# A hybrid encoder layer on one core: the down projection's first two tile pairs of each chunk interleaved, and the sums of the next feed-forward rows spread over four blocks

## The chip, the cores and the metric

One core of a Trainium2 chip runs the whole program. The metric is the device time in microseconds of one execution, as the median of several. The engines are TensorE (PE in the profile, its weight loads PEld), VectorE (DVE), ScalarE (ACT), GpSimd (POOL) and SyncE (SP), which here only issues transfers. Each works through its own instructions in order.

## The reference

One layer of a streaming encoder on 2176 rows (2048 of a prompt, 8 x 16 of running streams; 17 tiles of 128 rows), 1024 wide. A first half (a gated delta rule on four heads and a short convolution, with projections) ends in `x = x + RMSNorm(mix)`. The change concerns the second half:

```python
h = rmsnorm(x, norm_ffn_pre)
f = (jax.nn.silu(h @ w_gate) * (h @ w_up)) @ w_down      # 1024 -> 2816 -> 1024
x = x + rmsnorm(f, norm_ffn_post)
```

All is float32. The kernel splits each operand in a high part (a rounded copy) and a low part (the rest) and multiplies high x high, high x low and low x high.

## The kernel before

**Products.** Both projections of the feed-forward use Strassen's scheme in Winograd's form: two by two blocks with seven products in place of eight, bought with sums and differences of blocks.

**Gate and up.** The 17 tiles stand in three groups (`FGROUPS`: six, six and five tiles). For each group the rows are loaded (`ffn_load`, tiles `fh`), summed (`ffn_sums`, lines L1158, L1159 and, from the second group on, L1162, tiles `ft`) and split (`ffn_prep`, tiles `xh`, `xl`). Then come 22 blocks `f`, one for each 128 columns of gate and up: `gu_start` makes the first four products in four banks, `gate_up` copies them out on ScalarE (L1288 to L1290), makes the other three and forms silu(gate) times up on VectorE (L1296 to L1317). Every second block ends in sums for the down projection (`pt`, L1323 to L1326), which ScalarE's queue sends to memory (`partd`, L1328). The split weights `fw` of the next block are made alongside (L1220 to L1230) or, for later groups, partly read back (`fsplit`). Rows of the next group are loaded behind blocks 4 to 11 of the running one; its sums stand behind block 16 (`NF - 6`).

**Down.** The 22 blocks are the inner dimension of the down projection, in five chunks (`FCHUNKS`: four blocks four times, six at the end). In each chunk, eight tile pairs (`down_pair`) and the half tile pair left over (`down_single`) are multiplied with the chunk's weights; `acc` collects the five chunks' results. A pair has seven parts (`ar`, loaded by SP from `partd` in pieces of two, two and three parts; three buffers). Each part is split (`split`: L1399 the copy on ScalarE, L1402 the difference on VectorE or GpSimd; tiles `as`, six buffers) and multiplied (`product`, L1418; 6 matmuls, 9 in the last chunk) into one of four banks, each of which takes a second product after its first was brought out. Bringing out (`evac`) is a copy on ScalarE in the first chunk (L1451) and an addition on VectorE after it (`acc_add`, L1377). The eight banks go round (`fbank`).

The weights are prepared by a generator, `down_chunk`, one step at a time (`prep_step`): raw rows `dr` (L1084, four buffers), differences on VectorE (L1091 to L1097), and splits in a ring of 21 tiles `dw` (one of them `sA`, `sB`; L1108 the copy on ScalarE, L1110 the difference on VectorE or GpSimd). In a chunk of 14 weights, seven of the next chunk's are made in the middle; the steps for the others stand in its last pair, and the ring passes into the chunk after.

In the last chunk each pair ends in two differences (L1477, L1478) and two calls of `finish` (norm and residual): sums of squares on ScalarE (L1427), products with the gain (L1431), then the row scale and the residual (L1436), and the output.

**Order.** The framework's scheduler runs over the program with a timeline of its own (`TLS = True`), so an engine's final order is near the program's but not the same. `tc.issue_after` sets a lower bound for single instructions.

## Time and profile before

| | us |
|---|---|
| Median of 3 runs | 2518.31 (2517.99 to 2518.65) |
| The profiled execution | 2521.97 |
| its span, first to last instruction | 2520.1 |
| TensorE busy | 2464.6 |
| VectorE busy | 1612.6 |
| ScalarE busy | 1063.8 |
| GpSimd busy | 588.1 |
| First product of the down projection starts | 2036.9 |
| Its last products (48 matmuls from 2496.4) end | 2507.5 |

In the timeline's rows stand the start and the duration in us, the engine, the line, the operation, output and inputs, shapes, how many in a row were merged, and in brackets the idle time just before and what ended it. A row of the waits has the waiting engine, tile and line, whom it waited for, the total in us, how often, and the longest. A row of the windows has the stretch and its length, then for each engine the busy time and the number of instructions, then TensorE's granted clock (1 is full speed), the share of the transfer engines and GB/s. In a row of the groups the busy time and the mean in ns of one stand behind the first bar, idle time behind the second.

### The profile page before, as it was taken

The page shows a single profiled execution, that of the slowest core. Times are in us where ns is not written, and L with a number is a line of the kernel's source. Part 1 is how long each engine was busy: PE and PEld are TensorE (multiplying, and loading weights), DVE is VectorE, ACT ScalarE, POOL GpSimd, SP SyncE. Part 2 cuts the span into 40 slices and gives each one's busy share as a digit, 9 for nine tenths or more (in the row PEclk, how much of TensorE's full clock was granted, in tenths as well). Part 3 has the DMA queues.
Part 4 walks back from the last instruction along what each step waited for, and adds up shares of the span by engine and source line. Part 5 has one row for each costly group of instructions (what it writes and reads, how often), then busy time and mean ns, then how long its engine had stood idle before and what let it go on. Part 6 is the DMA issues. An engine that isn't in the chain of part 4 may idle for free. (4 is left out here: it accounts for less than half of the span.)

```text
span 2520.1 us, 39370 instructions
## 1 busy us (share of the span) xinstructions
PE 2464.6 (98%) x14366; PEld 2253.3 (89%) x14366; DVE 1612.6 (64%) x3025; ACT 1063.8 (42%) x2355; POOL 588.1 (23%) x663
## 2 busy tenths in 40 slices
PE   8999999999999999999999999999999999999997
PEld 7988888889999988789999999999999987887786
DVE  5966645645666555868878754455555564677688
ACT  5656445445435343534444422223333345333343
POOL 1101011011010001325665400000000055455564
PEclk9999999999999999999999999999999999999999
DMA  7855555456676556669876878878998743344465
GB/s 268 320 205 193 211 194 193 176 181 225 231 243 235 196 187 223 222 227 322 293 273 239 284 246 277 268 246 262 290 308 282 255 146 121 93 126 124 129 222 184
DMA packets 282498, 561.91 MB, mean 223 GB/s; under 512 B 26108, under 2 KB 174784, under 8 KB 265024
## 3 DMA queue, kind: packets, MB, share of 16 engines
q1 hardware_dynamic: 161200, 483.52, 56.6%
q10 hardware_dynamic: 121104, 75.88, 9.6%
q8 instruction: 113, 1.85, 0.3%
q14 instruction: 81, 0.66, 0.1%
HBM read 400.62 MB, written 158.70 MB: 222 GB/s over the span
## 5 line engine op out<-in xcount | busy, mean ns | idle before, releaser
L1254 PE MATMUL fbank<-xh,fw 128*128 128x384 f32 (+1 forms) x3696 | 898.9, 326 | 4.5 <-DVE ht L1055 2.0
L298 PE MATMUL dbank<-hi,w 128*128 128x384 f32 (+1 forms) x2240 | 671.9, 368 | 8.9 <-ACT w L277 6.0
L1254 PEld LDWEIGHTS fbank<-xh,fw 128*128 128x128 f32 x3696 | 651.9, 188 | 5.8 <-ACT m L1290 2.6
L1254 PE MATMUL fbank<-xl,fw 128*128 128x384 f32 (+1 forms) x1848 | 602.5, 326 | 0.0
L298 PEld LDWEIGHTS dbank<-hi,w 128*128 128x128 f32 x2240 | 416.7, 190 | 48.2 <-ACT w L277 6.2
L1418 PE MATMUL fbank<-dw,as 128*128 128x512 f32 x1884 | 445.2, 395 | 8.0 <-DVE as L1402 2.8
L1418 PEld LDWEIGHTS fbank<-dw,as 128*128 128x128 f32 x1884 | 355.2, 189 | 91.8 <-DVE acc L1377 4.1
L298 PE MATMUL dbank<-lo,w 128*128 128x384 f32 (+1 forms) x1120 | 402.2, 359 | 1.1 <-DVE lo L216 1.1
L1254 PEld LDWEIGHTS fbank<-xl,fw 128*128 128x128 f32 x1848 | 347.4, 188 | 0.0
L1402 POOL TENSOR_TENSOR as<-ar,as 128x256 fp32r<-128x256 f32 (+1 forms) x207 | 186.4, 911 | 230.1 <-ACT as L1399 227.0
L298 PEld LDWEIGHTS dbank<-lo,w 128*128 128x128 f32 x1120 | 212.9, 190 | 18.7 <-DVE lo L216 1.6
L1377 DVE TENSOR_TENSOR acc<-acc,fbank 128x512 f32<-128x512 f32 x248 | 166.3, 682 | 97.5 <-PE fbank L1418 83.4
L1399 ACT CAST as<-ar 128x256 fp32r<-128x256 f32 (+1 forms) x288 | 118.6, 427 | 187.1 <-PE fbank L1418 133.8
L1110 POOL TENSOR_TENSOR dw<-dr,dw 128x512 fp32r<-128x512 f32 x48 | 70.2, 1473 | 521.5 <-ACT dw L1108 521.4
L1229 ACT CAST fw<-rg 128x512 fp32r<-128x512 f32 x124 | 77.3, 623 | 187.8 <-PE fbank L1254 158.9
L302 DVE SCALAR_TENSOR_TENSOR acc<-R,cw,acc 128x384 f32<-128x384 f32 (+2 forms) x180 | 121.6, 677 | 53.0 <-ACT acc L332 44.4
L1301 DVE TENSOR_TENSOR c<-u,fbank 128x384 f32<-128x384 f32 (+1 forms) x66 | 34.9, 529 | 116.0 <-PE fbank L1254 116.0
L1299 ACT ACTIVATE m<-fbank 128x384 f32<-128x384 f32 (+1 forms) x66 | 31.3, 474 | 132.8 <-PE fbank L1254 131.8
L1297 DVE TENSOR_TENSOR m<-m,m 128x384 f32<-128x384 f32 (+1 forms) x44 | 23.1, 525 | 92.1 <-ACT m L1290 92.0
L1230 POOL TENSOR_TENSOR fw<-rg,fw 128x512 fp32r<-128x512 f32 x44 | 68.6, 1558 | 45.0 <-ACT fw L1229 44.8
L324 POOL COPY hist<-R 128x3 f32<-128x3 f32 x60 | 18.3, 305 | 255.1 <-ACT R L307 202.1
L1290 ACT COPY m<-fbank 128x384 f32<-128x384 f32 (+1 forms) x66 | 30.5, 461 | 88.5 <-PE fbank L1254 57.0
(362 smaller groups left out, 3573.6 us busy)
## 6 DMA issues: line engine op xcount, KB each, us to landing
w<-wsplit SPq DMA_DIRECT2D x105, 1024.0 KB, 5.1
fw<-fsplit SPq DMA_DIRECT2D x188, 512.0 KB, 4.6
fsplit<-fw SPq DMA_DIRECT2D x94, 512.0 KB, 3.9
partd<-pt ACTq DMA_DIRECT2D x88, 384.0 KB, 6.3
rg<-in_w_gu SPq DMA_DIRECT2D x62, 512.0 KB, 3.6
wsplit<-w SPq DMA_DIRECT2D x28, 1024.0 KB, 4.9
ar<-partd SPq DMA_DIRECT2D x48, 384.0 KB, 3.3
wr<-in_w_in SPq DMA_DIRECT2D x34, 512.0 KB, 5.9
```

Source lines behind the costliest of these rows:

```text
L298: T.matmul(ps[:, :c], l[:, k, :], r[k][:, :c], start=(k == 0 and r is hi and l is wh), stop=(k == KD - 1 and l is wl))
L302: r = V.scalar_tensor_tensor(acc, raw(d), w[:, d:d + 1], acc, op0=ALU.mult, op1=ALU.add)
L1110: e.tensor_tensor(out=w[1], in0=v, in1=w[0].bitcast(F32), op=ALU.subtract)
L1229: A.copy(w[:, 0], v)
L1230: e.tensor_tensor(out=w[:, 1], in0=v, in1=w[:, 0].bitcast(F32), op=ALU.subtract)
L1254: T.matmul(ps, w_[:, c], b_[k][:, :hw], start=(first and k == 0 and ci == 0), stop=(k == KH - 1 and ci == 2), skip_group_check=not first)
L1299: A.activation(sg0, b1, AF.Silu)
L1301: V.tensor_add(c21, u2, b3)
L1377: V.tensor_add(dst, dst, ps)
L1399: ins = A.copy(a[:, 0, :n], v)
L1402: e.tensor_tensor(out=a[:, 1, :n], in0=v, in1=a[:, 0, :n].bitcast(F32), op=ALU.subtract)
L1418: T.matmul(ps, a[:, x_, q * P:(q + 1) * P], w[y_], start=(start and q == 0 and ci == 0), stop=(q == c - 1 and ci == 2), skip_group_check=True)
```

## The change

It has two parts.

**The sums of the next rows.** `ffn_sums` now takes a range of `k`. In place of all four `k` behind block 16, one `k` (three operations for a later group) stands behind each of blocks 16 to 19.

**The pairs.** `down_pair` becomes a generator. For the first two pairs of a chunk (`duo`) it stops after its loads and after each product, and the loop takes turns: first pair's product, second pair's product with the same weights, and so on; in the first chunk two products of each come first. The two hold four banks each, so all eight. A pair's first four parts are then one load. The second pair's last three parts are loaded only ahead of its fourth product, since the three `ar` buffers are taken. In the first chunk all of the second pair's differences are on VectorE. The half pair, which stood behind the first pair, stands behind both, and in the last chunk the ends of both pairs (the two differences and `finish`) stand behind the fourteenth product. The rest of the pairs run as before.

```diff
-        def ffn_sums(gi, hs, fs):
+        def ffn_sums(gi, hs, fs, sums=None, ks=range(KH)):
             hw = len(FGROUPS[gi]) * P // 2
-            t3, t2 = [], []
-            for k in range(KH):
+            t3, t2 = sums or ([], [])
+            for k in ks:
...
-                    if f == NF - 6:
+                    if NF - 6 <= f < NF - 6 + KH:
                         with tc.issue_after(gmark["V"].ins):
-                            t3 = ffn_sums(gi + 1, hs, fd)
+                            t3 = ffn_sums(gi + 1, hs, fd, t3 if f > NF - 6 else None, [f - NF + 6])
...
+            duo = pairs.index(u) < 2
             ready = first_parts if (ch, u) == (0, pairs[0]) else []
-            parts = (ready or load_parts(src, 0, 2)) + load_parts(src, 2, 4) + load_parts(src, 4, 7)
+            if duo:
+                parts = ready + load_parts(src, len(ready), 4)
+                yield
+            else:
+                parts = load_parts(src, 0, 2) + load_parts(src, 2, 4)
+            if u != pairs[1]:
+                parts += load_parts(src, 4, 7)
...
-                product(b, ch, ready[i] if i < len(ready) else split(parts[i], V if i in ((0,) if end else (0, 3)) else G, bool(ready)), i, mid)
+                if i == 3 and len(parts) == 4:
+                    parts += load_parts(src, 4, 7)
+                e = V if i in ((0,) if end else (0, 3)) or (duo and not ch and not ready) else G
+                product(b, ch, ready[i] if i < len(ready) else split(parts[i], e, duo and not ch), i, mid)
...
-            cast.clear()
+                if duo:
+                    yield
             if end:
...
+            yield
...
-            for k, u in enumerate(pairs):
-                down_pair(ch, u, k == len(pairs) - 1)
-                if k == 0 and not end:
-                    down_single(ch, single)
-                elif 2 <= k <= 6:
+            duo = [down_pair(ch, u, False) for u in pairs[:2]]
+            for i in (0, 1, 0, 0, 1, 1) + (0, 1) * 5 if not ch else (0, 1) * 8:
+                next(duo[i])
+            for d in duo:
+                next(d, None)
+            cast.clear()
+            if not end:
+                down_single(ch, single)
+            for k, u in enumerate(pairs[2:], 2):
+                for _ in down_pair(ch, u, k == len(pairs) - 1):
+                    pass
+                if k <= 6:
                     prep_step(spare * (k - 1) // 5 - spare * (k - 2) // 5)
```

What this does to the order of instructions, at three places. VectorE behind block 16 of the first group (`ft` and `fh` are the sums and rows of the next group, `pt` the sums for the down projection, `fw` and `sD` weights); a row with a minus stood there before, one with a plus stands there now:

```order
 L1317 TENSOR_TENSOR a_13823<-m_13733,c_13817 128x384
 L1158 TENSOR_TENSOR ft_13827<-fh 128x384
-L1158 TENSOR_TENSOR ft_13832<-fh 128x384
-L1158 TENSOR_TENSOR ft_13837<-fh 128x384
-L1158 TENSOR_TENSOR ft_13842<-fh 128x384
 L1324 TENSOR_TENSOR pt<-a_13822,a_13823 128x384
-L1159 TENSOR_TENSOR fh<-fh 128x384 x4
+L1159 TENSOR_TENSOR fh<-fh 128x384
 L1162 TENSOR_TENSOR ft_13830<-fh 128x384
 L1230 TENSOR_TENSOR fw<-sD,fw 128x512
```

One sum of each kind is left there; the others stand in the same way behind L1317 of blocks 17, 18 and 19, among L1323 to L1326.

ScalarE at the start of the second chunk, before. `as` are the copies of parts from the loads `ar` (21555 and 21557 are the first pair's second and third load, 21633 the half pair's), `acc2_1` the last pair of the first chunk, `dw` weights of the third chunk from raw rows `dr`:

```order
L1399 CAST as_21583<-ar_21555 128x256
L1451 COPY acc2_1_21428<-fbank_21429 128x512
L1399 CAST as_21593<-ar_21555 128x256
L1451 COPY acc2_1_21428<-fbank_21430 128x512
L1399 CAST as_21603<-ar_21557 128x256
L1108 CAST dw_21530<-dr_21512 128x512
L1451 COPY acc2_1_21428<-fbank_21431 128x512
L1399 CAST as_21613<-ar_21557 128x256
L1399 CAST as_21623<-ar_21557 128x256
L1108 CAST dw_21543<-dr_21526 128x512
L1108 CAST dw_21547<-dr_21512 128x512
L1399 CAST as_21637<-ar_21633 128x256
```

The same stretch now, where `ar` 21551 is the first pair's first four parts, 21553 the second pair's, 21555 the first pair's last three:

```order
L1399 CAST as_21585<-ar_21551 128x256
L1451 COPY acc2_1_21426<-fbank_21427 128x512
L1399 CAST as_21595<-ar_21553 128x256
L1451 COPY acc2_1_21426<-fbank_21428 128x512
L1399 CAST as_21605<-ar_21551 128x256
L1108 CAST dw_21528<-dr_21510 128x512
L1451 COPY acc2_1_21426<-fbank_21429 128x512
L1399 CAST as_21615<-ar_21553 128x256
L1399 CAST as_21625<-ar_21551 128x256
L1108 CAST dw_21541<-dr_21524 128x512
L1399 CAST as_21637<-ar_21553 128x256
L1108 CAST dw_21545<-dr_21510 128x512
```

The copies alternate between the two pairs; the weight copies keep their places among them.

VectorE in the last chunk at the end of the first pair, before (`acc0_0` is the first pair, `acc0_1` the second, `gpo` the gain, `fss2` and `f2m` steps of the norm):

```order
L1377 TENSOR_TENSOR acc0_0_20767<-acc0_0_20767,fbank_23778 128x512
L1377 TENSOR_TENSOR acc0_1_20912<-acc0_1_20912,fbank_23913 128x512
L1477 TENSOR_TENSOR acc0_0_20767<-acc0_0_20767 128x512
L1377 TENSOR_TENSOR acc0_0_20767<-acc0_0_20767,fbank_23779 128x512
L1402 TENSOR_TENSOR as_24051<-ar_24041,as_24051 128x384
L1478 TENSOR_TENSOR acc0_0_20767<-acc0_0_20767 128x512
L1377 TENSOR_TENSOR acc0_1_20912<-acc0_1_20912,fbank_23914 128x512
L1428 TENSOR_TENSOR fss2_23876<-fss2_23876 128x1
L1431 TENSOR_TENSOR acc0_0_20767<-acc0_0_20767,gpo_21550 128x512
```

And now (L1488 and L1489 are the former L1477 and L1478):

```order
L1377 TENSOR_TENSOR acc0_0_20769<-acc0_0_20769,fbank_23764 128x512
L1488 TENSOR_TENSOR acc0_0_20769<-acc0_0_20769 128x512
L1377 TENSOR_TENSOR acc0_1_20788<-acc0_1_20788,fbank_23781 128x512
L1488 TENSOR_TENSOR acc0_1_20788<-acc0_1_20788 128x512
L1377 TENSOR_TENSOR acc0_0_20769<-acc0_0_20769,fbank_23765 128x512
L1489 TENSOR_TENSOR acc0_0_20769<-acc0_0_20769 128x512
L1377 TENSOR_TENSOR acc0_1_20788<-acc0_1_20788,fbank_23782 128x512
L1428 TENSOR_TENSOR fss2_23959<-fss2_23959 128x1
L1431 TENSOR_TENSOR acc0_0_20769<-acc0_0_20769,gpo_21548 128x512
L1489 TENSOR_TENSOR acc0_1_20788<-acc0_1_20788 128x512
```

The ends of both pairs stand together, where before the first pair's stood among the second pair's first additions.

## The prediction

> **What bounds the kernel now.** I read the page first, then the waits of TensorE, then windows of 10 us around each wait, and at those places the timeline.

> ```profile
> PE 2464.6 (98%) x14366; PEld 2253.3 (89%) x14366; DVE 1612.6 (64%) x3025; ACT 1063.8 (42%) x2355; POOL 588.1 (23%) x663
> PE fbank L1418 <- DVE as L1402: 2.8, 2, 2.6
> PE fbank L1418 <- DVE acc L1377: 2.0, 2, 1.3
> PE fbank L1418 <- ACT dw L1108: 1.4, 1, 1.4
> PE fbank L1418 <- POOL dw L1110: 0.6, 2, 0.4
> PE fbank L1418 <- DVE accs L1377: 0.5, 1, 0.5
> PE fbank L1418 <- DVE dw L1110: 0.4, 2, 0.2
> PE fbank L1418 <- ACT as L1399: 0.2, 1, 0.2
> PE fbank L1254 <- ACT m L1290: 2.0, 2, 1.8
> PE fbank L1254 <- ACT m L1288: 0.6, 1, 0.6
> ```

> TensorE is busy for 98%, so only its own waits can be won. The rows give the total wait, the count and the longest. L1418 is the down stage: 7.9 us, all at the starts of its five chunks. L1254 is gate/up; of its 2.6 us, 0.2 lies elsewhere, and 2.3 lie in one block near 1390 us (1.8 and 0.6, less rounding). A wait has a second price:

> ```profile
> 1397.00:1403.00 6.00, 4.93 (x19) 4.93 (x20) 5.26 (x6) 3.55 (x7) 4.85 (x4) 0.72 0.97 327
> 2044.00:2055.00 11.00, 8.45 (x30) 6.47 (x31) 8.63 (x11) 5.57 (x11) 10.59 (x9) 0.84 0.65 207
> 2134.00:2141.00 7.00, 5.71 (x18) 4.19 (x18) 7.00 (x10) 2.33 (x6) 3.85 (x4) 0.76 0.34 95
> 2386.00:2394.00 8.00, 6.64 (x21) 5.06 (x22) 7.92 (x10) 3.82 (x7) 4.86 (x4) 0.79 0.37 121
> 1128.00:1138.00 10.00, 8.64 (x52) 8.03 (x50) 9.49 (x12) 4.47 (x10) 7.31 (x6) 1.00 1.01 374
> ```

> The third number from the right is the granted clock. The missing share times the window is 6 x 0.28, 11 x 0.16, 7 x 0.24 and 8 x 0.21, each 1.7 us: after the longest wait of that place TensorE loses 1.7 us to a slow spell. The last row has idle time too (8.64 of 10 busy) and a full clock, so not every wait brings a spell. The stake is thus 2.3 + 1.7 = 4.0 us in gate/up and 7.9 + 3 x 1.7 = 13.0 us in the down stage, 17.0 together.

> **Part one, the sums of the next rows.** Twelve VectorE operations stood in one burst; now three stand behind each of four blocks.

> ```profile
> 1373.53 4.97 DVE L1158 TENSOR_TENSOR ft<-fh 128x384 f32<-128x384 f32 x4
> 1381.84 1.48 DVE L1162 TENSOR_TENSOR ft<-fh 128x384 f32<-128x384 f32 x3
> 1333.59 0.69 DVE L1230 TENSOR_TENSOR fw<-sD,fw 128x512 fp32r<-128x512 f32 x1 [2.93 <-ACT fw L1229]
> 1351.46 1.26 DVE L1220 TENSOR_TENSOR sC<-rg,ru 128x512 f32<-128x512 f32 x1 [1.76 <-DMA ru<-in_w_gu]
> 1333.46 0.47 ACT L1290 COPY m<-fbank 128x384 f32<-128x384 f32 x1
> 1362.64 0.47 ACT L1290 COPY m<-fbank 128x384 f32<-128x384 f32 x1
> 1398.07 0.44 PE L1254 MATMUL fbank<-xh,fw 128*128 128x384 f32 x1 [1.77 <-ACT m L1290]
> ```

> One sum takes 0.49 us alone (1.48 / 3) and 1.24 beside GpSimd (4.97 / 4), so a quarter takes 1.5 to 3.7 us. Two blocks last 29.2 us (the two L1290 copies), and in them VectorE has idle stretches of 2.93 and 1.76 us. Two quarters, 3.0 to 7.4 us, against 4.7 of idle time: at the middle they fit. Slack of the L1290 copy: TensorE wanted it at 1398.07 - 1.77 = 1396.3, less the 0.6 it had already lost; two periods earlier, 1337.3. There the copy ended at 1333.9, so it has 3.4 us. A quarter in the chain L1317 to L1326 delays the partd issue on ScalarE, behind which L1290 stands, by 1.5 to 3.7; the cast of sD now goes ahead of that issue. I take the middle, 2.6, so the wait and its spell go. If the quarter comes at 3.7, 0.3 is left in a block. **Gain 3.5, between 0 and 4.0.** For the second group VectorE is half idle and nothing waits now; nothing is gained there. The loads of rows (fh) keep their blocks.

> [...]

> **Part two, interleaved pairs.** No matmul, split or sum is added: 42 matmuls a pair remain, and one load issue per interleaved first pair goes, as two become one.

> ```profile
> 2080.33 0.39 PE L1418 MATMUL fbank<-sA,as 128*128 128x512 f32 x1
> 2090.02 0.39 PE L1418 MATMUL fbank<-sA,as 128*128 128x512 f32 x1
> 2129.01 0.62 ACT L1108 CAST dw<-dr 128x512 fp32r<-128x512 f32 x1 [2.94 <-DMA dr<-in_w_dn]
> 2133.32 1.77 DVE L1093 TENSOR_TENSOR dr<-dr 128x512 f32<-128x512 f32 x1
> 2135.75 1.25 PE L1418 MATMUL fbank<-dw,as 128*128 128x512 f32 x3 [1.29 <-DVE acc L1377]
> 2382.18 0.62 ACT L1108 CAST dw<-dr 128x512 fp32r<-128x512 f32 x1 [2.57 <-DMA dr<-in_w_dn]
> 2386.47 1.34 ACT L1108 CAST dw<-dr 128x512 fp32r<-128x512 f32 x2 [3.25 <-DVE dr L1091]
> ```

> A pair lasts 9.69 us, a product 1.38. At the start of chunk 1 TensorE waits 1.29 us for a bank: the fifth product of a pair reuses the bank of the first, four products (5.5 us) on, and the adding into acc that frees it stands in VectorE's queue behind weight preparation (L1093, 1.77). With eight banks the reuse is eight products (11 us) away, so this wait goes, with its spell. At the start of chunk 4 TensorE waited 1.4 us for a weight that was held by a load (2.57) and by VectorE (3.25); with two pairs the same weights feed twice the matmuls, 2.8 us more per weight index, which covers it.

> What the change does not touch: ScalarE still takes a weight cast in order ahead of the splits, and stands until the load has landed. And the second pair's last load (parts 4 to 6) is issued only when the first pair's fourth part is split, since there are three ar buffers; behind it on SP stand the loads of the single tile and of the next pair.

> Start by start, with what was lost before (waits, and 1.7 where there is a spell):
> - Chunk 0: 5.1 (DVE as 2.6, POOL dw 0.6, one DVE dw 0.2, a spell). New waits, from these rows:

> ```profile
> 2039.68 0.92 DVE L1326 TENSOR_TENSOR pt<-pt 128x320 f32<-128x320 f32 x1
> L1402 POOL TENSOR_TENSOR as<-ar,as 128x256 fp32r<-128x256 f32 (+1 forms) x207 | 186.4, 911 | 230.1 <-ACT as L1399 227.0
> L1399 ACT CAST as<-ar 128x256 fp32r<-128x256 f32 (+1 forms) x288 | 118.6, 427 | 187.1 <-PE fbank L1418 133.8
> L1110 POOL TENSOR_TENSOR dw<-dr,dw 128x512 fp32r<-128x512 f32 x48 | 70.2, 1473 | 521.5 <-ACT dw L1108 521.4
> ```

>   The second pair's first split now stands on VectorE behind L1326, which ended at 2040.6; TensorE is there two products after its start, at 2039.7, so some 0.8 us. GpSimd then has a split (0.91) between weight subtractions (1.47), 1 us over its four products' time; I take 1.8 in all, no spell. Back: 3.3.
> - Chunk 1: 3.2 (ACT as 0.2, acc 1.3, a spell). The as casts held by ScalarE leave some 0.8. Back: 2.4.
> - Chunks 2 (acc 0.7) and 3 (DVE as 0.2, accs 0.5): back 0.5 each.
> - Chunk 4: 3.3 (ACT dw 1.4, DVE dw 0.2, a spell). The late load of the second pair may leave 1.0. Back: 2.3.

> **Gain 9.0, between 0 and 13.0** (below 0 in the first rival).

> **Part three, the last chunk.** There each pair ends with finish (norm and residual). The first pair's ran beside the second pair's products; now both come behind the fourteenth product.

> ```profile
> 2416.00:2508.00 92.00, 91.48 (x397) 73.90 (x396) 85.55 (x147) 35.58 (x91) 46.22 (x44) 1.00 0.68 215
> L1377 DVE TENSOR_TENSOR acc<-acc,fbank 128x512 f32<-128x512 f32 x43 | 28.5, 676 | 0.1
> L1436 DVE SCALAR_TENSOR_TENSOR xr<-acc,f2r,xr 128x512 f32<-128x512 f32 x30 | 27.9, 967 | 0.5
> L1431 DVE TENSOR_TENSOR acc<-acc,gpo 128x512 f32<-128x512 f32 x27 | 19.0, 705 | 3.9 <-ACT junkd L1427 3.9
> L1477 DVE TENSOR_TENSOR acc<-acc 128x512 f32<-128x512 f32 x7 | 6.2, 881 | 0.2
> L1478 DVE TENSOR_TENSOR acc<-acc 128x512 f32<-128x512 f32 x7 | 5.3, 762 | 0.2
> ```

> A pair's finish is four L1436, four L1431, L1477 and L1478: 3.9 + 2.8 + 0.9 + 0.8 = 8.4 us, of which operations overlap a little; I count 8.2. After 2416 us VectorE has 92 - 85.6 = 6.4 us idle left, of which 3.9 is waiting for ScalarE. So 8.2 go into at most 6.4: VectorE ends 1.8 late at best, 8.2 at worst. Banks hide it from TensorE (a bank is needed again 4 x 2.1 us later, and an acc takes 0.68), but the final rows do not. **Loss 3.0, between 0** (GpSimd's share may shift and free the 0.2 in each L1436) **and 8.2.**

> **Sum.** 3.5 + 9.0 - 3.0 = 9.5 us less. The profiled execution took 2521.97 us (span 2520.1), 3.7 over the median 2518.31; the difference is made against it and carried to the median: 2508.8.

> **Rivals.**
> First, slower: *the late fourth load*. Place: the second pair's parts 4 to 6, at starts 1 to 4.

> ```profile
> ar<-partd SPq DMA_DIRECT2D x8, 576.0 KB, 4.2
> ```

> At start 1 the hold ended at 2129.0; a weight cast and a copy (0.6 each), two casts (0.43 each) and a split (0.9) bring the first pair's fourth part to 2132.0. Landing (at most 4.2), cast and split make 2137.5. TensorE began the chunk at 2126.0 (2090.02 is the third product of the fifth pair: three pairs and 6.9 us more) and wants the part nine products on, at 2138.4. That leaves 0.9 us; from there on every us that ScalarE is held longer is a wait. With start 4's two holds on top (2.57 + 3.25), 4.9 us and a spell of 1.7 at each of four starts are 26 us in place of 7.9 lost before: 3.5 + 3.3 - 18 - 3.0, 14 slower, 2532.5. For it: ScalarE's order is kept. Against: the weight casts held there follow on fewer splits. Chance 0.13.

> Second, *order, not weight rate*: the waits come from ScalarE's queue and not from banks, and are only moved. Then only the bank waits (2.0 and a spell, 3.7) and gate/up (3.5) come back, less 3.0: 4.2 less, 2514.1. For it: the scheduler's order before already had the single tile and the second pair between the first pair's products. Against: the longest wait at chunk 1 is a bank. Chance 0.15.

> Third, *the spells stay*. Four of them, 6.8 us, are in my gains. If they come for another reason, 2.7 are left: 2515.6. For it: the window at 1128 us, idle without a spell. Against: four spells, each just after a place's longest wait. Chance 0.07. [...]

> Fourth, *VectorE's surplus is not absorbed* in the last chunk at all, 8.2, with two spells of 1.7: 3.5 + 9.0 - 11.6 = 0.9 less, 2517.4. Chance 0.05.

> **How the numbers follow.** My forecast has 0.60. What this kernel's measurement can tell from no change is about 0.2%, 5 us. Faster: 0.58 of my case, 0.06 of the second rival (its gain is 4.2, near the bound), 0.02 of the third: 0.66. Slower: the first rival 0.13, a part of the fourth and what I have not seen 0.05: 0.18. The rest, 0.16, is the same. The range leaves out the first rival, takes in the second to fourth, and below takes all stakes but 0.7 of the 17.0: 2502 to 2519.

> **What would show it.** Right: no wait on ACT m near 1390 us and a clock of 1.00 there; no wait on acc at chunk starts; TensorE's L1418 waits under 4 us in total; VectorE above 95% after 2416 us. Wrong: waits at products 5 and 6 of the second pair released by as or ar; new slow spells; or a L1290 wait in two or three blocks in place of one.

## The result, and the profile after

The kernel after takes 2515.24 us in the median (2509.52 to 2521.70, 22 runs), the kernel before 2518.93 (2516.55 to 2522.40, 22 runs) in the same session: ratio 0.9983, 95% interval [0.9977, 0.9990], 3.7 us less where 9.5 were forecast. The profiled execution of after took 2510.25 us (span 2508.5), 5.0 under its own median, while that of before stood 3.0 over its own. The two traces therefore differ by 11.7 us, three times what the medians differ by. Of the 11.7 us, 1.3 lie ahead of gate/up, where both kernels are the same, 3.1 in gate/up, 6.6 in the down stage and 0.7 behind it. A comparison of these two traces alone would have confirmed the forecast, and it would have been wrong.

The page of after (busy time of the engines) and its waits of TensorE in gate/up (L1254) and down (L1418), with total, count and longest:

```profile
PE 2456.3 (98%) x14366; PEld 2246.8 (90%) x14366; DVE 1609.8 (64%) x3030; ACT 1059.8 (42%) x2355; POOL 592.7 (24%) x658
PE fbank L1418 <- DVE acc L1377: 2.3, 4, 1.1
PE fbank L1418 <- DVE as L1402: 2.0, 3, 1.2
PE fbank L1254 <- ACT m L1289: 0.9, 1, 0.9
PE fbank L1418 <- POOL as L1402: 0.8, 2, 0.5
PE fbank L1418 <- ACT as L1399: 0.8, 1, 0.8
PE fbank L1254 <- ACT m L1290: 0.3, 1, 0.3
```

The dw waits of before are gone, the long single waits too; what is left at L1418 is 5.9 us in ten pieces, where 7.9 stood. Windows of after at the places that the prediction showed (window, length, busy time of PE, PEld, DVE, ACT and POOL, granted clock, DMA share, GB/s):

```profile
1385.00:1400.00 15.00, 15.00 (x88) 15.00 (x87) 11.03 (x17) 5.35 (x11) 7.18 (x5) 1.00 0.74 257
1448.00:1456.00 8.00, 7.08 (x41) 6.76 (x40) 7.47 (x16) 2.38 (x5) 0.00 (x0) 1.00 0.65 191
2040.00:2055.00 15.00, 12.49 (x52) 9.19 (x51) 14.85 (x18) 9.91 (x24) 11.01 (x10) 1.00 0.58 194
2130.00:2145.00 15.00, 14.71 (x63) 11.34 (x62) 14.90 (x23) 5.54 (x14) 11.57 (x10) 1.00 0.33 97
2376.00:2391.00 15.00, 15.00 (x67) 12.16 (x66) 10.86 (x15) 7.45 (x15) 12.99 (x12) 1.00 0.42 137
2416.00:2497.00 81.00, 78.97 (x342) 63.44 (x340) 76.94 (x132) 30.73 (x79) 42.55 (x39) 1.00 0.69 222
```

The clock is 1.00 at all of them: the four spells (stretches at half clock) of before are not there. The first chunk (third row) still loses 2.5 us in waits, a new 0.92 us stands near 1451 us, and the last chunk loses 2.0.

Since single executions scatter this much, three stretches are compared below over all traces of a kind: gate/up from the first L1254 matmul to the first L1418 one, the down stage from there to the end of the last, and the tail behind it. Each experiment left one trace, and that execution need not be a typical one: e5's took 11.9 us more than its kernel's median, e4's 6.3 and e1's 5.2 more, after's 5.0 and e9's 4.7 less. What stands ahead of gate/up, and is the same in all, took 1112.6 to 1121.0 us. The late difference and the load buffer are edits of the experiments below.

| Kernels | gate/up, us | down stage, us | tail, us |
|---|---|---|---|
| sums in a burst (before twice, e2, e10) | 922.2, 922.0, 922.3, 921.4: mean 922.0 | | |
| spread sums (after twice, e1, e3, e4, e6, e8, e9) | 919.1, 924.2, 923.9, 923.4, 927.0, 920.3, 921.2, 919.4: mean 922.3 | | |
| spread sums, late difference (e5, e7, e11, e13 to e16) | 917.2 to 919.6: mean 918.2 | | |
| no interleaving (before twice, e1, e10, e11) | | 470.7, 470.6, 467.3, 471.3, 467.1: mean 469.4 | 12.5 to 12.6 |
| interleaved in all chunks, nothing else in the down stage (after twice, e2) | | 464.1, 464.9, 464.8: mean 464.6 | 11.9 to 12.0 |
| the same with the late difference (e5, e13, e15) | | 469.1, 467.9, 467.9: mean 468.3 | 11.9 |
| the same with the late difference and the load buffer (e7, e14, e16) | | 464.3, 465.3, 465.0: mean 464.9 | 11.9 to 12.0 |

### The profile page after: what moved, and what is told of

It is laid out like the page before. It is cut to its first block, busy times and chain, and to the rows that moved or that the text cites. A ratio compares the mean times of both kernels' runs of the same rounds, so it can differ in the third digit from the quotient of the medians.

```text
span 2508.5 us, 39356 instructions
## 1 busy us (share of the span) xinstructions
PE 2456.3 (98%) x14366; PEld 2246.8 (90%) x14366; DVE 1609.8 (64%) x3030; ACT 1059.8 (42%) x2355; POOL 592.7 (24%) x658
## 3 DMA queue, kind: packets, MB, share of 16 engines
q8 instruction: 113, 1.85, 0.3%
## 4 chain that ended last, share of the span: by engine, by line
PE 79%; DVE 10%; DMA 4%; ACT 4%; issue 2%; POOL 1%; ACTq 0%; SPq 0%; DVEq 0%; POOLq 0%
PE fbank L1254 34%; PE dbank L298 20%; PE fbank L1418 11%; PE tbank L1031 3%; PE dbank L1031 3%; DMA wr<-in_w_in 2%; DVE acc L1377 1%; DVE acc L302 1%; DVE xr L1436 1%; DVE xl L1182 1%; DVE w L278 1%; PE tbank L343 1%; PE obank L694 1%; PE gbank L749 1%; PE gbank L702 1%
## 5 line engine op out<-in xcount | busy, mean ns | idle before, releaser
L1254 PE MATMUL fbank<-xh,fw 128*128 128x384 f32 (+1 forms) x3696 | 897.5, 326 | 3.2 <-DVE ht L1055 2.0
L1254 PEld LDWEIGHTS fbank<-xh,fw 128*128 128x128 f32 x3696 | 651.1, 188 | 4.2 <-DVE ht L1055 2.3
L1254 PE MATMUL fbank<-xl,fw 128*128 128x384 f32 (+1 forms) x1848 | 601.9, 326 | 0.0
L1418 PE MATMUL fbank<-dw,as 128*128 128x512 f32 x1884 | 441.4, 392 | 6.0 <-DVE acc L1377 2.3
L1418 PEld LDWEIGHTS fbank<-dw,as 128*128 128x128 f32 x1884 | 352.1, 188 | 89.3 <-DVE acc L1377 4.0
L1254 PEld LDWEIGHTS fbank<-xl,fw 128*128 128x128 f32 x1848 | 346.9, 188 | 0.0
L1402 POOL TENSOR_TENSOR as<-ar,as 128x256 fp32r<-128x256 f32 (+1 forms) x202 | 183.7, 920 | 230.2 <-ACT as L1399 227.9
L1377 DVE TENSOR_TENSOR acc<-acc,fbank 128x512 f32<-128x512 f32 x248 | 165.0, 682 | 90.5 <-PE fbank L1418 77.2
L1399 ACT CAST as<-ar 128x256 fp32r<-128x256 f32 (+1 forms) x288 | 117.1, 427 | 185.0 <-PE fbank L1418 115.4
L1110 POOL TENSOR_TENSOR dw<-dr,dw 128x512 fp32r<-128x512 f32 x48 | 70.4, 1477 | 511.6 <-ACT dw L1108 511.3
L1229 ACT CAST fw<-rg 128x512 fp32r<-128x512 f32 x124 | 77.3, 623 | 185.9 <-PE fbank L1254 164.2
L1230 POOL TENSOR_TENSOR fw<-rg,fw 128x512 fp32r<-128x512 f32 x44 | 69.2, 1573 | 44.5 <-ACT fw L1229 44.4
L1290 ACT COPY m<-fbank 128x384 f32<-128x384 f32 (+1 forms) x66 | 30.5, 462 | 99.8 <-PE fbank L1254 69.0
```

The costliest lines, as they stand in the source:

```text
L1110: e.tensor_tensor(out=w[1], in0=v, in1=w[0].bitcast(F32), op=ALU.subtract)
L1229: A.copy(w[:, 0], v)
L1230: e.tensor_tensor(out=w[:, 1], in0=v, in1=w[:, 0].bitcast(F32), op=ALU.subtract)
L1254: T.matmul(ps, w_[:, c], b_[k][:, :hw], start=(first and k == 0 and ci == 0), stop=(k == KH - 1 and ci == 2), skip_group_check=not first)
L1377: V.tensor_add(dst, dst, ps)
L1399: ins = A.copy(a[:, 0, :n], v)
```

## The experiments

### One part alone, and before once more (e0 to e3)

e1 puts the spread sums of the diff into before; e2 takes them out of after:

```diff
-                    if NF - 6 <= f < NF - 6 + KH:
+                    if f == NF - 6:
                         with tc.issue_after(gmark["V"].ins):
-                            t3 = ffn_sums(gi + 1, hs, fd, t3 if f > NF - 6 else None, [f - NF + 6])
+                            t3 = ffn_sums(gi + 1, hs, fd)
```

e3 keeps the pairs of the last chunk one after the other (`duo = pairs.index(u) < 2 and not end`); e0 is before.

> The kernel before, unchanged, for a second trace and for the scatter of the comparison. A ratio of 1.000 within 0.001. If the waits and spells of the first trace are typical (theory A): waits at L1418 of about 8 us in total, on ACT m of 2 us near 1390, and four spells of half clock after 1050 us. By theory B fewer: a total of waits and spells 5 us or more lower.

> The kernel before with the spread sums alone (pairs one after the other, as before). Theory A, the terms of the prediction hold: gate/up gives back 3.5 us (waits of 2.3 and a spell of 1.7 near 1390 us go), so some 3.5 us under before. Theory B, the profiled execution of before was not typical (it stood 3.0 over its median, the one after 5.0 under its own, so that the two traces differ by 11.7 and the medians by 3.7): the stake that is lost in most executions is about a third of what the trace showed, and the sums give some 1.2 us. Theory C, the sums do nothing by themselves and the pairs bring all: within 0.5 us of before. In the profile: no wait on ACT m near 1390 us by A and B.

> The kernel after with the twelve sums back in one burst: the interleaved pairs alone. Theory A: 9.0 less 3.0, some 6.0 us under before. Theory B (a third of the stake is typical): some 2.5 us under. Theory C (the pairs bring all): 3.7 us under, like the kernel after. In the profile by A and B: the wait on ACT m of about 2 us near 1390 us is there again, with or without a spell; the starts of the chunks as in the kernel after.

> The kernel after without the interleaving in the last chunk (there pairs one after the other, each with its finish, as before). Theory A with the last chunk's loss mis-sized at its other end, 8.2 us in place of 3.0: this kernel is 8 us faster than the kernel after, some 12 under before. Theory B: the last chunk costs what the trace of after shows, two waits on acc of 0.51 and 1.07 us, less what chunk 4 had lost before (waits 1.6 and a spell 1.7): within 1.7 us of the kernel after on either side. Were the start of the last chunk the one place where the interleaving wins, it would be 2 to 3.3 us slower than the kernel after.

Measured, against a common median of before of 2519.65 us (33 runs):

| Kernel | us | ratio |
|---|---|---|
| e0 before again | 2520.23 | 1.0002 [0.9993, 1.0011] |
| e1 spread sums alone | 2516.40 | 0.9990 [0.998, 1.0] |
| e2 pairs alone | 2517.59 | 0.9991 [0.9982, 1.0] |
| e3 after, last chunk as before | 2515.67 | 0.9988 [0.9979, 0.9996] |

Each part brings some 2 to 3 us, neither all of it; both intervals reach 1.000, so either part alone is barely told from no change. Every run comes with its mean granted clock, so its time can be divided into what the clock took (1 less the clock, times the time) and the rest. Averages over the runs: before 17.9 and 2502.2, e1 17.9 and 2500.0, e2 15.1 and 2502.1, after 15.1 and 2499.9 (its own session), each uncertain by 0.4 to 1.0 (the clock is on record in steps of 0.001, 2.5 us of the time, so only averages can be read). In these averages the sums save no clock, and the pairs save little else.

Theory B falls in its first form: e0's trace has the same four spells and 7.9 us of waits at L1418. The stake was no accident of one execution. But it was not certain either: e1, whose pairs are those of before, has only the first of the three spells in the down stage, though its waits there are again 7.9 us. That is taken up under the spells.

e3's time is that of after (2515.24, and 2515.80 in e12). The last chunk's interleaving thus did not cost 8.2 us.

### The first chunk only, twice (e4, e8), and the others only (e9)

e4 turned the interleaving off in chunks 1 to 4 with `duo = pairs.index(u) < 2 and ch == 0`, but left the single tile behind both pairs, where the diff had put it. e8 puts it back between the first and the second pair in those chunks; e9 does the reverse of e8 (`ch > 0`).

```diff
+            for k, u in enumerate(pairs):
+                if k < 2 and DUO(ch):
+                    continue
...
+                if k == 0 and not end:
+                    down_single(ch, single)
```

> The kernel after with the interleaving in the first chunk alone (spread sums kept; in the other four chunks pairs one after the other). Theory S, what the pairs win is spells and hardly waits: TensorE idle at the starts of chunks 1 to 4 is again about 4.5 us (1.3 on acc, 1.4 on dw among it), and the spells behind chunk starts 1 and 4 are there in about half of the executions; the time is 1.5 to 2.5 us over the kernel after. Theory W (the prediction's): the waits themselves were won, 3.3 us of them at chunks 1 to 4: 4 to 6 us over the kernel after. In the first chunk both expect the four pieces of wait of the kernel after, 3.3 us in all, none above 1.3, and no spell.

> Spread sums; the first chunk interleaved; the other four chunks wholly as before, the single tile between the first and the second pair again (which the run with the first chunk only had not put back). Theory S, the pairs win spells and hardly waits: in the first chunk about 3.3 us of waits in pieces and no spell, in the others the waits of before (4.5 us) with their spells; 0.5 to 2 us faster than the spread sums alone, 3 to 4.5 under before. Theory W of the prediction: first chunk 3.3 us, so 5.8 to 6.8 under before. If the position of the single tile, and not the interleaving, made the run with the first chunk only slow (6.5 over before), the waits at chunk starts 1 to 3 are those of before here, some 2.8 us, and not 10.6.

> Spread sums; the first chunk as before, the other four interleaved. Theory S: the wait of 2.6 us and its spell stay in the first chunk, the spells at chunks 1 and 4 go, the waits there go from 4.5 us to 2.5 with the late finish of the last chunk among them: 1 to 3 us faster than the spread sums alone, 3.5 to 5.5 under before. Theory W: 5.7 less 3.0 gained besides the sums, about the same 2.7. The two differ in what is seen: by S all of it is spells and 2 us of waits, and the end costs nothing.

e4 takes 2526.14 us, ratio 1.0026 [1.0015, 1.0038]: slower than before by 6.5, which no theory had expected. The timeline of e4's TensorE at the start of chunk 1 (start, duration, and in brackets the idle time ahead and its releaser), then the one wait of e8 there:

```profile
2138.54 1.20 PE L1418 MATMUL fbank<-dw,as 128*128 128x512 f32 x4 [1.67 <-ACT as L1399]
2141.01 0.97 PE L1418 MATMUL fbank<-dw,as 128*128 128x512 f32 x3 [1.27 <-DVE acc L1377]
2148.78 1.20 PE L1418 MATMUL fbank<-dw,as 128*128 128x512 f32 x4 [1.14 <-DVE as L1402]
2151.21 3.25 PE L1418 MATMUL fbank<-dw,as 128*128 128x512 f32 x13 [1.23 <-DVE acc L1377]
```

```profile
2133.33 0.97 PE L1418 MATMUL fbank<-dw,as 128*128 128x512 f32 x3 [1.06 <-DVE acc L1377]
```

Over chunks 1 to 3 e4 waits 10.6 us and e8 2.3, on the same pairs one after the other. So the single tile's place was worth some 8 us with the pairs one after the other. With them interleaved its place behind both costs nothing that the traces show: in after twice and e2, chunks 1 to 3 wait 1.0 to 1.8 us. e4 was thus no clean undo. e8 takes 2515.70 us, 0.9982 [0.9973, 0.9992]; e9 2516.22, 0.9986 [0.9975, 0.9997]. Either part with the spread sums comes out like the whole change (0.9983), and the times don't rank them.

The traces do tell what each start won. Waits of TensorE, interleaved against not, over all traces of the kernels in the table's rows "no interleaving" and "nothing else in the down stage", e3, e8 and e9: chunk 0 3.2 to 4.0 against 3.4 to 3.7; chunk 1 0.2 to 0.5 against 1.1 to 2.4; chunk 2 up to 0.4 against 0.5 to 0.7; chunk 3 0.7 to 0.9 against 0.5 to 1.3; the start of chunk 4 nothing against 1.7; further on in the last chunk 1.6 to 1.8 against 0 to 0.7.

### The difference that stands for a transfer (e5, e10, e11)

With the spread sums all three traces so far had a wait of TensorE on ACT m near 1455 us that before does not have (0.92 us in after, 1.40 in e1, 2.95 in e3). In the second trace of after (e12, below) it is 2.56 us; VectorE's timeline ahead of it, and the wait:

```profile
1429.66 0.56 DVE L1317 TENSOR_TENSOR a<-m,c 128x384 f32<-128x384 f32 x1
1430.13 0.55 DVE L1182 TENSOR_TENSOR xl<-fh,xh 128x384 fp32r<-128x384 f32 x1
1437.65 0.56 DVE L1324 TENSOR_TENSOR pt<-a,a 128x384 f32<-128x384 f32 x1 [6.96 <-DMA partd<-pt]
1455.59 0.45 PE L1254 MATMUL fbank<-xh,fw 128*128 128x384 f32 x1 [2.56 <-ACT m L1289]
```

L1324 writes pt, which the last transfer to partd is still reading: VectorE stands 6.96 us for its landing, and behind it in its queue are the splits of the next rows (L1182) and the next block's chain, for whose L1317 ScalarE's L1289 waits. In before, L1317 came later (1432.73) and L1324 followed at 1433.67 without a wait:

```profile
1432.73 0.56 DVE L1317 TENSOR_TENSOR a<-m,c 128x384 f32<-128x384 f32 x1
1433.67 0.55 DVE L1324 TENSOR_TENSOR pt<-a,a 128x384 f32<-128x384 f32 x1
```

That it came later is the smaller half of the difference. The three transfers that read pt ahead of it (L1328, near 1422 us in both traces) took, from issue to landing, in before and then in e12:

```profile
DMA to landing us min/median/max: 3.5/6.1/7.5
DMA to landing us min/median/max: 2.8/8.5/14.1
```

The last of the three took 7.3 to 7.7 us in before, e0 and e2, and 12.8 to 15.3 us in all sixteen other traces. Issued at 1423.43 in e12 and landed after 7.5 us, it would have held L1324, which was free to start at 1430.69, for 0.2 us.

The edit holds L1324 back in the last block of a group, on after (e5), on before (e10), and on before with the spread sums (e11):

```diff
-                V.tensor_sub(pt[:, 1, :hw], a11, a21)
+                with tc.issue_after(gmark["V"].ins) if f == NF - 1 else ExitStack():
+                    V.tensor_sub(pt[:, 1, :hw], a11, a21)
```

> The kernel after with one VectorE operation in the last block of each group of rows (the difference written to the second row of pt, L1324) held behind L1317 of that block. Theory P: with the sums spread, this operation reaches VectorE 3 us earlier than before, and the queue stands behind it 5.3 to 8.0 us until the last transfer from pt to partd has landed; so the split of the next rows comes late, and TensorE waits 0.9 to 3.3 us on ACT m near 1455 us. Then without it: no wait of VectorE on partd near 1435 us, the wait near 1455 under 0.5, gate/up at 919 us or under, and the time 1 to 3 us under the kernel after. Rival Q: the wait near 1455 comes from the amount of VectorE work at the change of groups, not from the transfer: it stays at 1 us or more, and the time is that of the kernel after within 1 us.

> The kernel before with the late difference alone (sums in one burst, pairs one after the other). Theory P (the difference stands in VectorE's way only when the sums are spread and it comes 3 us earlier): nothing to win, ratio 1.000 within 0.001. Rival: the edit is worth its 3 us by itself, since the wait on partd would also be there in many executions of before: 2 to 4 us faster.

> The kernel before with the spread sums and the late difference, without interleaving. Theory P: the waits on ACT m at 1390 and 1455 us are both under 0.7, gate/up takes 918 to 920 us (922 in before, 924 with the spread sums alone), and the gain is what the prediction gave the sums, 3.5 us, and up to 5 with the transfer out of the way. Rival Q: 1455 stays at 1 us or more and the gain is the 2 to 2.5 us of the spread sums alone.

e5: 2511.49 us (7 runs), 0.9962 [0.9948, 0.9976]; e10: 2518.61, 0.9991 [0.998, 1.0002], not told from no change; e11: 2516.91, 0.9985 [0.9976, 0.9994]. In e5 and e11 the wait near 1455 us is gone and gate/up takes 919.6 and 919.2 us. Theory P holds for the wait: it comes from the stand for the transfer. Its reason, that L1324 comes 3 us earlier, does not hold in all traces: in e1 that block's L1317 comes as late after the start of gate/up as in before (318.1 and 318.0 us), and VectorE stands 5.80 us all the same, since the transfer took 14.5. What makes the transfer land later is open; e10, whose sums stand in one burst, has 15.0 too, and no run separates it. The gain in time over the spread sums alone is smaller in e11 than expected (0.9985 against 0.9990, inside both intervals); against before it is 3.9 us, what the prediction gave the sums. One piece is not explained: near 1397 us e11 still waits 1.40 us on ACT m L1290, as e1, e3, e4 and e12 do (1.4 to 1.8) and e5 with 0.70; after's first trace, e6 to e9 and e13 to e16 don't.

### The load of the second pair (e6, e7)

Chunk 0's waits did not shrink. ScalarE's and TensorE's timelines of after there:

```profile
2045.67 0.71 ACT L1399 CAST as<-ar 128x256 fp32r<-128x256 f32 x2 [3.35 <-DMA ar<-partd]
2046.13 1.42 PE L1418 MATMUL fbank<-dw,as 128*128 128x512 f32 x5 [0.81 <-ACT as L1399]
2048.77 3.37 PE L1418 MATMUL fbank<-dw,as 128*128 128x512 f32 x13 [1.22 <-DVE as L1402]
2052.62 11.86 PE L1418 MATMUL fbank<-dw,as 128*128 128x512 f32 x50 [0.47 <-DVE as L1402]
```

ScalarE stands 3.35 us for a load that SP could issue only when one of the three ar buffers was free. e6 adds a buffer, e7 is e5 and e6 together:

```diff
-            a = da.tile([P, 4, MC * P // 2], F32, tag="ar", name="ar", bufs=3)
+            if hi - lo == 2 and (lo == 0 or not acc):
+                a = da.tile([P, 2, MC * P // 2], F32, tag="ar2", name="ar2")
+            else:
+                a = da.tile([P, 4, MC * P // 2], F32, tag="ar", name="ar", bufs=3)
```

> The kernel after with one more buffer of two parts for the loads of hidden products (loads of two parts at a pair's or the single tile's start, and the first pair's third and fourth part in the first chunk, take it). Theory L: in the first chunk the waits of TensorE (0.81, 1.22, 0.47) come from the second pair's last load, issued only when a buffer was free, for which ScalarE stood 3.35 us. With a free buffer the load is issued some 10 us earlier: ScalarE does not stand there, the three waits shrink from 2.5 us to under 0.8, and the time is 1.5 to 2.5 us under the kernel after. Rival V: VectorE's queue (weight preparation, 1.8 us each) is what makes the splits late: waits of 2 us or more stay in the first chunk, and the time is that of the kernel after within 1 us.

> The two edits together, the late difference and the further load buffer, on the kernel after. If theories P and L hold, the gains add: 3 to 5 us under the kernel after, 7 to 9 under before (2511). If only one of them holds, 1.5 to 2.5 us under the kernel after. If neither, the time of the kernel after within 1 us.

e6: 2513.79 us, 0.9970 [0.996, 0.9981]; e7: 2509.78 (6 runs), 0.9957 [0.9945, 0.9968]. ScalarE's stand for partd is gone in e6, but the next one takes its place (e6's longest wait of ScalarE between 2030 and 2075 us, then TensorE's timeline in the first chunk):

```profile
ACT dw L1108 <- DMA dr<-in_w_dn: 4.4, 2, 3.7
```

```profile
2048.22 12.52 PE L1421 MATMUL fbank<-dw,as 128*128 128x512 f32 x52 [0.96 <-ACT dw L1108]
2062.72 2.07 PE L1421 MATMUL fbank<-dw,as 128*128 128x512 f32 x4 [1.98 <-ACT as L1399]
```

Besides a 0.32 at its start this is 3.3 us again, so theory L is wrong on the waits. V forecast that they stay, but for another reason: ScalarE now stands for the rows of the down weights to land, not for VectorE. With the load issued 16 us earlier (2024.87 in e6, 2040.59 in after) the next transfer is what is late. The gain in time of e6 over after (0.9970 against 0.9983, intervals overlapping) is not shown by its trace.

### The versions on one chip (e12 to e14), and the edit in two groups (e15, e16)

> The kernel after, unchanged, on one chip with the next two. If gate/up at 919.05 us in its first trace was luck (the mean of seven traces with spread sums is 922.0): 920 to 924 us here, VectorE standing 5 us or more for partd near 1435, a wait of 0.9 to 3.3 us near 1455. If it is what this kernel does: 919 again. Time 3 to 5 us under before.

> The kernel after with the late difference, again. Theory P: gate/up 917 to 920 us, no wait of TensorE over 0.7 near 1455, and 2 to 3 us faster than the kernel after of this call. Rival Q: the same time as the kernel after within 1 us, the earlier distance being that of seven runs.

> The late difference and the further load buffer, again. By P with the load buffer's gain (the second us or two from shorter waits and fewer spells at the starts): 4 to 6 us under the kernel after of this call, 8 to 10 under before. If the load buffer is worth nothing: the time of the kernel with the late difference alone, within 1 us.

After again 2515.80 us, 0.9981 [0.9971, 0.9990]; late difference 2513.70 (7 runs), 0.9971 [0.9960, 0.9983]; both 2510.34 (5 runs), 0.9962 [0.9949, 0.9974]. After's second trace has 924.24 us in gate/up: the 919.05 of the first was luck, the lowest of the eight traces of its row. The late difference has 918.5 and 917.8. Windows at the two places, of after again and then of e13:

```profile
1392.00:1399.00 7.00, 5.37 (x31) 5.05 (x31) 4.66 (x9) 2.83 (x6) 2.36 (x2) 1.00 0.81 264
1452.00:1460.00 8.00, 5.43 (x22) 5.12 (x22) 7.20 (x15) 2.40 (x5) 0.00 (x0) 0.79 0.65 197
```

```profile
1392.00:1399.00 7.00, 7.00 (x42) 7.00 (x42) 4.75 (x9) 2.53 (x6) 2.15 (x3) 1.00 0.83 263
1448.00:1456.00 8.00, 8.00 (x48) 8.00 (x48) 5.94 (x13) 1.87 (x4) 0.00 (x0) 1.00 0.67 202
```

e13 and e5 have a wait of about 2.3 us with a spell in the first chunk instead, and their down stages take 467.9 and 469.1 us: in these traces the down stage loses about what gate/up wins. The timeline of e13's TensorE:

```profile
2071.26 5.06 PE L1419 MATMUL fbank<-dw,as 128*128 128x512 f32 x14 [2.28 <-DVE acc L1378]
```

The edit also acts in the last group, whose last block runs into the down stage. e15 and e16 (with the load buffer) leave it out there: `f == NF - 1 and gi + 1 < len(FGROUPS)`.

> The kernel after with the late difference only in the first two groups of rows, where a next group's rows follow. If the 2.3 us wait on acc in the first chunk (near 2072 us) of the two traces with the late difference comes from its use in the last group, whose block runs into the down stage: gate/up 918 to 919 us as with the late difference, the down stage at 464 to 465 us as in the kernel after with no wait over 1.3 us in the first chunk, and 1.5 to 3 us faster than the late difference in all groups, 7 to 9 under before. If not: the 2.3 us wait stays, down stage 468 or more.

> The same with the further load buffer. If the load buffer only made up for the late difference in the last group: no faster than the kernel without it, within 1 us. If it has a gain of its own: 1 to 2 us faster, 9 to 11 under before.

e15: 2512.34 us (7 runs), 0.9968 [0.9957, 0.9979]; e16: 2512.53 (6 runs), 0.9967 [0.9955, 0.9979]. In e15 the 2.3 us wait is gone (longest in the first chunk 1.20) and gate/up takes 918.2, but the down stage is 467.9; chunk 1 now waits 2.1 us, where after and e2 wait 0.2 to 0.5. The rest of that loss, and what in the late difference brings it, is open. In time e15 and e13 are not told apart. The load buffer adds nothing to the time here, though the three traces with it have the down stage back at 464.9 in the mean. The two edits together in the form of e7 and e14 gave the lowest times of all, 0.9957 and 0.9962: 9 to 10 us under before, some 5 under after, measured twice on different chips; their intervals overlap those of e5, e6 and e13.

### When a wait brings a spell

The traces record when TensorE's granted clock changes. In before and after all twelve spells ahead of the last matmul last 3.413 us or 6.827, and within a trace they start whole multiples of 3.413 us apart, on one grid. Counted from the span's start, the grid lies at 2.92 us in before and at 1.64 in after. The same wait of chunk 0 in before and in e9, in windows cut on that grid of each:

```profile
2040.68:2044.10 3.42, 2.62 (x9) 1.25 (x8) 3.42 (x3) 3.17 (x9) 3.27 (x3) 1.00 0.69 208
2044.10:2047.51 3.41, 1.41 (x6) 0.77 (x5) 3.41 (x4) 1.45 (x3) 3.41 (x3) 1.00 0.68 206
2047.51:2050.92 3.41, 2.86 (x7) 2.28 (x8) 3.41 (x5) 2.21 (x5) 3.41 (x4) 0.50 0.36 110
```

```profile
2039.03:2042.45 3.42, 1.93 (x8) 1.05 (x6) 3.42 (x3) 1.82 (x5) 3.42 (x4) 1.00 0.71 193
2042.45:2045.86 3.41, 1.92 (x8) 1.60 (x9) 3.41 (x5) 2.56 (x5) 3.41 (x4) 1.00 0.39 138
2045.86:2049.27 3.41, 3.41 (x16) 2.74 (x16) 2.65 (x4) 1.30 (x3) 3.41 (x4) 1.00 0.70 216
```

The waits are the same, 2.55 us and 2.57. In before 2.0 us of idle time fall into one window (PE 1.41 of 3.41), and the next runs at 0.50; in e9 the grid cuts the wait so that two windows are idle for 1.49 us each, and nothing follows. Over all 19 traces, from 1100 us on, windows by the idle time of TensorE in them: 1.85 us or more, 11 of 11 were followed by half clock; 1.45 to 1.85, 10 of 33; 1.0 to 1.45, none of 60; below, one of 7,685 (itself at half clock). This is a count over traces; no run set a wait's length by hand.

## Why the prediction missed

- **Gate/up sums, 3.5 forecast.** Measured: nothing in gate/up (922.3 against 922.0 us in the traces), 2.2 us in the average time of e1. The step that failed is where the moved work stalls and what is late next. The prediction named the partd issue on ScalarE, but not that VectorE writes pt again and must stand for that transfer's landing; it put this at nothing. VectorE stood 5.3 to 8.0 us there in the traces of after, e1, e3 and e12. Counted from the start of gate/up, the chain came 2.4 us earlier in e12, 4.3 in after's first trace and not at all in e1; the larger part is the landing, 12.9 to 15.1 us after the issue in these four and 7.5 in before. With L1324 moved out of the way gate/up falls by 3.7 (918.2): the size of the term was right, its path was not. For the bound of 0 the prediction shows no reading, though the traces' result lies on it; the quarters last 3.5, 2.7, 4.6 and 1.6 us in the trace of after (lengths of three operations added), where 1.5 to 3.7 was estimated.
- **Interleaved pairs, 9.0 forecast, 6.0 with the last chunk's 3.0 taken off.** Measured, last chunk and tail included: 5.4 us in the traces (469.4 to 464.6 and 0.6 in the tail), 2.9 in the average time of e2. The two are not reconciled: e2's traced execution itself stood 2.9 under that average, so the traces flatter. Two terms failed. The waits: 4.0 of 7.9 were to stay; 5.9 to 6.5 stay, 1.6 of them in the last chunk. Chunk 0 was forecast at 1.8 and has 3.2 or more: the late load of the first rival stands there, at the one start that the rival left out, and with that load out of the way (e6) the down weights' rows take its place at 3.3. The spells: all three of before's trace were counted as certain, 5.1 us; in five traces without interleaving there are 9 of 15 possible, 3.1 us a run. Only one of the three windows had 1.85 us of idle time or more; the other two, with 1.49 and 1.65, lie where 10 of 33 windows brought a spell.
- **Banks and weights** were read rightly: at chunk 1 the wait on acc falls from 1.3 to 0.2, at chunk 4 the wait on a weight goes, with their spells.
- **The last chunk, 3.0 lost.** It lost less than that: the deferred finishes reach TensorE as 0.51 and 1.07 us on acc,

```profile
2441.33 13.32 PE L1418 MATMUL fbank<-dw,as 128*128 128x512 f32 x56 [0.51 <-DVE acc L1377]
2457.54 2.83 PE L1418 MATMUL fbank<-dw,as 128*128 128x512 f32 x11 [1.07 <-DVE acc L1377]
```

  and the tail is 0.6 shorter. VectorE's busy share after 2416 us rose from 93% to 95% as forecast (76.94 of 81). In the last 81 us before the same point, 2427 to 2508, before has 74.65, so the deferral brought 2.3 us more into them and not 8.2. Nothing of it came out behind the last matmul; what did not fit became a wait of TensorE. "Banks hide it from TensorE" was the false sentence.
- **The carry to the median.** Stakes read from one execution were taken off the median as if every execution had its spells. Of the three in the down stage, e1's trace has one, e10's two and e11's none.
- **The rivals.** In time the third (the spells stay: 2515.6) and the second (order, not weight rate: 2514.1) came nearest, both by luck. The third is refuted by three traces of the interleaved down stage without a spell; the second by the waits at chunk 4 that it kept, which are gone. The first, the late load, is there at chunk 0 alone, with 2.5 us of waits behind it and not 26. The fourth fails with e3, whose time is that of after.
- **The signs to look for**: the clock of 1.00 near 1390 us and VectorE's 95% came true; the wait near 1390 came back in after's second trace (1.63), with a new spell at 1456, one of the signs of being wrong; L1418 waits stayed at 6 us, not under 4.

## To carry to other kernels

Before work is moved forward on an engine, look at which buffer its next write reuses and whether the transfer that reads it will have landed by then; here the new wait stood there, and the landing itself moved by 5 us and more (from 7.3 to 7.7 us after the issue to 12.8 to 15.3). In these traces a wait cost its length and sometimes a spell, 1.7 us each in before. Half clock followed 11 of 11 windows of the grid with 1.85 us of idle time or more, 10 of 33 with 1.45 to 1.85 and none of 60 with 1.0 to 1.45. So a wait broken into pieces of 1.2 us won the spell though no wait was saved: chunk 0 waits 3.4 us in before, with a spell, and 3.2 to 3.6 in after and e2, without. Where a kernel scatters by several us, take a second trace of each before a difference of traces is believed.
